# A two-layer hybrid decoder trunk on one core: mixer weights of layer 1 made ready in layer 0's feed-forward stage and kept in DRAM, and a mask added by a transfer

## The chip, the cores and the metric

The kernel runs on one core of one Trainium2 chip. Its time is the device time of one execution in microseconds (us). The profile gives, for one execution, the span from the first to the last instruction, what each engine did, and the clock that was granted to TensorE. The engines are named as in the profile: PE (TensorE matmuls), PEld (its weight loads), DVE (VectorE), ACT (ScalarE), POOL (GpSimd), SP (SyncE, which here only issues DMAs).

## The reference, cut to what matters

Two layers, each on 512 positions of width 1024, all in float32:

```python
h = rmsnorm(x, mix_pre_g[i])
z = h @ w_in[i]                      # 3206 columns: gMLP u, v | retention q, k, v, gate | FoX q, k, v, forget
...                                  # three mixers: spatial gating, retention (6 heads), forgetting attention (6 heads)
mix = concat([out_a, out_b, out_c]) @ w_o[i]
x = x + rmsnorm(mix, mix_post_g[i])
h = rmsnorm(x, ffn_pre_g[i])
g = h @ w_gate[i]                    # 1024 x 4096
act = gelu(causal_conv3(g)) * (h @ w_up[i])
x = x + rmsnorm(act @ w_down[i], ffn_post_g[i])
x = x + rmsnorm((p[i] @ w_ple_proj) * sigmoid(rmsnorm(x) @ w_ple_gate), ple_post_g[i])
```

In the forgetting attention the score of query t and key s gets the difference of two running sums of the log forget gates, and keys after the query are masked out. `log_f` is summed along the sequence by head; a row of these sums is added to the scores.

## The kernel before, in words

**Precision and the products.** A float32 matrix is cut into a high part (a cast on ACT) and a low part (the difference, on DVE); `split` does one such pair of instructions. A product then takes three matmuls on PE: high by high, high by low, low by high.

**Seven products for eight.** The feed-forward stage's gate and up projections, and 14 of the column blocks of `w_in`, are worked in pairs. Two blocks of 128 weight columns (g and u) by two halves of the contraction, against two halves of the tokens, would be eight block products; `seven` does it with seven, on sums of blocks. Each of the seven is 4 x 3 = 12 matmuls of 256 columns that go into the PSUM tiles `beta` and `ag`. `seven_weights` makes a pair ready: it loads 1 MiB into the tile `graw` (four pieces u2, u1, g1, g2 of 128x512), splits g into `wg` and u2 into `wu`, adds the pieces to each other, and splits the sums into `wsa` and `wsb`. Two of the four additions are made by DMAs that POOL issues and that add in flight, two by DVE:

```python
G.dma_start(out=u1, in_=src[:, 0, :], accum_op=ALU.add)   # u1 += u2, from DRAM
G.dma_start(out=g1, in_=src[:, 1, :], accum_op=ALU.add)   # g1 += u1, from DRAM
for t, by in ((u2, g1), (g2, u2)):                        # on DVE
    V.tensor_tensor(out=t, in0=t, in1=by, op=ALU.add)
```

The results of `seven` leave PSUM by ACT copies into `gs`/`us` (in the mixers `fqk`, `rm`, and a part of a `mix` tile) and by DVE additions. PE goes on accumulating in the same bank, so a product waits for the eviction of the one before the last.

**The stages.** For each layer: the mixers (layer 0 about 28 to 215 us, layer 1 about 808 to 985 us in the profile), the output projection, the feed-forward stage of 32 blocks of gate and up with the down projection (`dn`) woven in from block 4 (layer 0 about 250 to 723 us, layer 1 from 1030 us), and the per-layer embedding with its gate (723 to 808 us in layer 0). In a layer's mixers seven pairs are worked: three for the retention's q and k (`r0` to `r2`), three for the forgetting attention's (`f0` to `f2`), and one for two blocks of the retention's gate (`g`).

**What sets the order.** No loop of the program is the order of execution. Every instruction is recorded with its dependences; `Plan.issue` then plays the recording through with a cost for each instruction and writes down, for each engine, the order in which it would start. This order is fixed at build time. Among ready instructions the one recorded first goes first. `AHEAD` says for each stage how far ahead of the oldest unfinished instruction a tile may be taken; `STEPS` and `O_ORDER` set the order in which the mixers and the blocks of the output projection are recorded. Large tiles (8 KB in each partition) come from 24 places in two sets, 15 of `X` and 9 of `W`; `wg`, `wsa` and `wsb` live in `W`.

**The forget mask.** For a pair of heads, `fox_proj` loads a head's row of sums from DRAM to all partitions (`fcb`), and DVE makes the masked copy by adding a 128x128 mask of 0 and 1e30 to each of its four 128-column pieces. `fox_attend` uses the plain half for whole blocks and the masked half for the diagonal ones.

Of the kernel before, what the change touches and what calls it, by code (L numbers as in the profile page):

```python
# [28 lines left out]
F32 = mybir.dt.float32  # L29
# [7 lines left out]
P = 128  # L37
# [13 lines left out]
class Plan:  # L51
# [10 lines left out]
    AHEAD = {"mix": 422, "wo": 488, "wo2": 330, "emb": 950, "gu0": 403, "gu": 478, "dn": 1080, "end": 351, "pg": 618, "pg2": 206}  # L62
# [407 lines left out]
def constants():  # L470
# [16 lines left out]
    c["mask"] = np.where(idx[None, :] <= idx[:, None], 0.0, 1e30)  # L487
# [43 lines left out]
def body(ctx, tc, a, out):  # L531
# [26 lines left out]
    def b8(name, shape, dt=F32):  # L558
        kind = "W" if name in ("wg", "wsa", "wsb") else "X" if dt == F32R else None
        return b8t([P] + list(shape), dt, name, kind)  # L560
# [4 lines left out]
    def dram(name, shape):  # L565
        return dpt(list(shape), F32, tag=name, name=name, bufs=1)
# [263 lines left out]

    def seven_weights(src, dma=SUMS_BY_DMA):

# [3 lines left out]
        wg = b8("wg", (2, 1024), F32R)  # L836
# [11 lines left out]
        sa = b8("wsa", (2, 1024), F32R)  # L848
        split(sa[:, 0, :], sa[:, 1, :], raw[:, 0:1024])
        sb = b8("wsb", (2, 1024), F32R)  # L850
# [84 lines left out]
    def mixers(l, hT, uv, ready):  # L935
# [10 lines left out]
        mask = m5[:, 512:640]  # L946
        cosT = m5[:, 1536:2048]
        decay, qdec, cum, sinT = m6[:, 0:768], m6[:, 768:1152], m6[:, 1152:1408], m6[:, 1408:1920]
        for t, n in ((decay, "decay"), (qdec, "qdec"), (cum, "cum"), (mask, "mask")):
            SY.dma_start(out=t, in_=a["c_" + n])  # L950
# [95 lines left out]
        def fox_proj(p):  # L1046


            k, q = wk("fqk"), wk("fqk")
            seven(hT, seven_weights(a["w_fm"][l, 3 + p]), k, q, -0.125)  # L1050
# [44 lines left out]
        def ret_gates():  # L1095
            seven(hT, seven_weights(a["w_fm"][l, 6]), sg[:, 0, :], sg[:, 1, :])
# [6 lines left out]
        def ret_proj(p):  # L1103
            res = [wk("rm") for _ in range(2)]
            seven(hT, seven_weights(a["w_fm"][l, p]), *res)
# [138 lines left out]
    def ffn(l, hs, emb, ready, x, new, g, nxt):  # L1244
# [75 lines left out]
        for b in range(31):  # L1320
# [3 lines left out]
            gate_up(b, lambda: pieces(b))  # L1324
        plan.fence(False)
# [194 lines left out]
```

## Time and profile before

| | |
|---|---|
| time, 3 runs | 1572.74 us median (1572.61 to 1574.72) |
| the profiled execution | 1572.24 us, span 1570.5 us |
| PE | busy 1547.5 us, 10554 matmuls |
| DVE, ACT, POOL | busy 1219.3, 895.5, 229.6 us |
| DMA | 239.04 MB, of it 219.94 MB read from HBM and 17.33 MB written |

The time of the profiled execution is 1.7 us above its span. Almost all instructions come from one line (L451), because `Plan.issue` issues the recording; so the profile is read by tiles, not by lines. Busy shares are of the whole span; the stages have different limits, and what PE waits for in one of them is seen in a table by stage and in the rows of its timeline.

### The profile page before, as it was taken

To read this page: it belongs to the slowest core of one execution; us is meant where nothing else is said; L and a number is where in the kernel's file an instruction comes from. 1 tells how busy PE (TensorE), PEld (TensorE's weight loads), DVE (VectorE), ACT (ScalarE), POOL (GpSimd) and SP (SyncE) were. 2 spreads that over 40 slices of the span, in tenths; PEclk is the share of its full clock that TensorE was granted. 3 is DMA by queue.
4 is the path that set the end of the run, shared out by engine and by line. 5 is a ranking of instruction groups with operands and counts; after the bars stand their busy time and mean duration, and the time that the engine had idled before them with its cause. 6 is when DMAs were issued, how large, how long until landed. Compare 5 with 4: busy or idle time off the path is not lost. (4 is left out here: it accounts for less than half of the span.)

```text
span 1570.5 us, 27064 instructions
## 1 busy us (share of the span) xinstructions
PE 1547.5 (99%) x10554; PEld 1403.7 (89%) x10554; DVE 1219.3 (78%) x1985; ACT 895.5 (57%) x1505; POOL 229.6 (15%) x307
## 2 busy tenths in 40 slices
PE   8999999999999999999999999999999999999997
PEld 6998878999999999998889897799999999999986
DVE  6779978977778778768595699799677778778693
ACT  7548647755545545545583576586655545555462
POOL 2011023110110110102230201221011011011031
PEclk9999999999999999999999999999999999999999
DMA  9345618735644654555563546295545565464741
GB/s 331 73 121 123 239 31 251 204 95 154 153 116 130 170 131 109 166 156 206 216 162 101 122 112 202 81 287 124 158 108 155 147 164 120 121 176 100 251 165 54
DMA packets 87881, 239.04 MB, mean 152 GB/s; under 512 B 10036, under 2 KB 18364, under 8 KB 87752
## 3 DMA queue, kind: packets, MB, share of 16 engines
q1 hardware_dynamic: 64856, 195.81, 36.7%
q0 software_dynamic: 22464, 40.90, 16.1%
q8 instruction: 83, 1.36, 0.4%
q10 hardware_dynamic: 432, 0.59, 0.1%
q14 instruction: 46, 0.38, 0.1%
HBM read 219.94 MB, written 17.33 MB: 151 GB/s over the span
## 5 line engine op out<-in xcount | busy, mean ns | idle before, releaser
L451 PE MATMUL dn<-thl,act 128*128 128x512 f32 x1536 | 370.3, 391 | 0.0
L451 PEld LDWEIGHTS dn<-thl,act 128*128 128x128 f32 x1536 | 280.4, 188 | 52.3
L451 POOL DMA_DIRECT2D graw<-in_w_gu_dram x128 | 112.0, 891 | 756.7 <-DVE wg L451 470.8
L451 PE MATMUL ps<-thl,hT 128*128 128x512 f32 (+3 forms) x984 | 208.9, 368 | 0.3 <-DVE hT L451 0.3
L451 PEld LDWEIGHTS ps<-thl,hT 128*128 128x128 f32 x984 | 175.4, 188 | 24.1 <-DVE nm L451 0.8
L451 DVE TENSOR_TENSOR thl<-traw,thl 128x1024 fp32r<-128x1024 f32 (+3 forms) x124 | 141.9, 1153 | 14.1 <-ACT thl L451 13.9
L451 ACT CAST thl<-traw 128x1024 fp32r<-128x1024 f32 (+3 forms) x124 | 122.1, 1000 | 35.3 <-PE dn L451 24.1
L451 PE MATMUL beta<-hh,wu 128*128 128x256 f32 x936 | 123.1, 281 | 1.3 <-DVE us L451 1.3
L451 PEld LDWEIGHTS beta<-hh,wu 128*128 128x128 f32 x936 | 119.3, 189 | 5.6 <-DVE us L451 1.5
L451 PE MATMUL ag<-hhd,wsa 128*128 128x256 f32 x936 | 121.4, 278 | 2.7 <-DVE fqk L451 1.1
L451 DVE TENSOR_TENSOR wsb<-graw,wsb 128x1024 fp32r<-128x1024 f32 x78 | 95.3, 1221 | 35.3 <-PE beta L451 29.4
L451 PE MATMUL beta<-hh,wsa 128*128 128x256 f32 x936 | 121.1, 278 | 0.9 <-ACT gs L451 0.8
L451 PE MATMUL beta<-hh,wsb 128*128 128x256 f32 x936 | 120.1, 277 | 0.1
L451 PEld LDWEIGHTS ag<-hhd,wsa 128*128 128x128 f32 x936 | 113.0, 188 | 4.3 <-DVE gs L451 2.2
L451 DVE TENSOR_TENSOR graw<-graw 128x512 f32<-128x512 f32 x156 | 106.7, 686 | 12.9 <-DMA graw<-in_w_gu_dram 10.2
L451 PEld LDWEIGHTS beta<-hh,wsa 128*128 128x128 f32 x936 | 113.0, 188 | 2.0 <-ACT gs L451 1.5
L451 DVE TENSOR_TENSOR wg<-graw,wg 128x1024 fp32r<-128x1024 f32 x78 | 95.3, 1222 | 23.6 <-ACT wg L451 20.4
L451 PEld LDWEIGHTS beta<-hh,wsb 128*128 128x128 f32 x936 | 113.1, 188 | 0.5 <-ACT gs L451 0.3
L451 ACT CAST wsa<-graw 128x1024 fp32r<-128x1024 f32 x78 | 82.0, 1051 | 49.0 <-DVE wsb L451 25.8
L451 ACT CAST wg<-graw 128x1024 fp32r<-128x1024 f32 x78 | 82.1, 1054 | 42.3 <-PE ag L451 32.4
L451 DVE TENSOR_TENSOR wsa<-graw,wsa 128x1024 fp32r<-128x1024 f32 x78 | 95.3, 1222 | 11.7 <-ACT wsa L451 11.4
L451 DVE SCALAR_TENSOR_TENSOR cv<-gs,cw,cv 128x511 f32<-128x511 f32 (+1 forms) x128 | 95.3, 745 | 10.2 <-ACT cv L451 9.6
(220 smaller groups left out, 2677.3 us busy)
## 6 DMA issues: line engine op xcount, KB each, us to landing
graw<-in_w_gu_dram SPq DMA_DIRECT2D x128, 512.0 KB
graw<-in_w_gu_dram POOLq DMA_DIRECT2D x128, 256.0 KB, 5.6
traw<-in_w_dn_dram SPq DMA_DIRECT2D x64, 512.0 KB
x<-x SPq DMA_DIRECT2D x40, 512.0 KB
graw<-in_w_fm_dram SPq DMA_DIRECT2D x28, 512.0 KB
traw<-in_w_wo_dram SPq DMA_DIRECT2D x16, 512.0 KB
traw<-in_w_pg_dram SPq DMA_DIRECT2D x16, 512.0 KB
graw<-in_w_fm_dram POOLq DMA_DIRECT2D x28, 256.0 KB, 4.7
```

Of the source, the lines that this page charges most:

```text
L451: made = o[1](*[self.map(v) for v in o[2]], **{k: self.map(v) for k, v in o[3].items()})
```

## The change

For the seven pairs of layer 1's mixers, `keep` makes the weights ready while layer 0's feed-forward stage runs, after the recording of its blocks 5, 8, 11, 14, 17, 20 and 23, in tiles of its own (`keepwg`, `keepwsa`, `keepwsb`, and two `wu`). All four additions are on DVE there. Five stores put the result into DRAM, 3.5 MiB for a pair. In layer 1's mixers `pair_weights` loads these 3.5 MiB straight into `wg`, `wsa`, `wsb` and `wu`, where layer 0 still loads 1 MiB, adds and splits. The masked copy of a forget row is now made by a second load of the row and a DMA issued by POOL that adds the mask (128x512, four copies side by side) from DRAM; this is in both layers. `AHEAD`, `STEPS` and `O_ORDER` have new values, which act on the whole program.

```diff
-    AHEAD = {"mix": 422, "wo": 488, "wo2": 330, "emb": 950, "gu0": 403, "gu": 478, "dn": 1080, "end": 351, "pg": 618, "pg2": 206}
+    AHEAD = {"mix": 392, "wo": 1620, "wo2": 330, "emb": 291, "gu0": 480, "gu": 368, "dn": 2187, "end": 2406, "pg": 1806, "pg2": 221, "keep": 972}
...
-STEPS = "u F H f0 g f1 a0 v r0 a1 G s r1 L r2 c0 f2 a2 c1 c2"
+STEPS = "u H F f0 g f1 a0 v r0 a1 G s r2 r1 L c0 c2 f2 a2 c1"
-O_ORDER = (5, 6, 0, 1, 2, 7, 3, 4)
+O_ORDER = (5, 6, 0, 1, 2, 4, 7, 3)
+KEEP = (5, 8, 11, 14, 17, 20, 23)
...
+    def pair_weights(l, p):
+        if (l, p) not in kept:
+            return seven_weights(a["w_fm"][l, p])
+        big, wud = kept[l, p]
+        ws = [b8(n, (2, 1024), F32R) for n in ("wg", "wsa", "wsb")]
+        for t, src in zip(ws, big):
+            SY.dma_start(out=t.bitcast(F32), in_=src)
+        wu = [wk("wu", dt=F32R) for _ in range(2)]
+        for t, src in zip(wu, wud):
+            SY.dma_start(out=t.bitcast(F32), in_=src)
+        return ws[0], wu, ws[1], ws[2]
+
+    def keep(l, p):
+        wg, wu, sa, sb = seven_weights(a["w_fm"][l, p], kind="keep", dma=False)
+        big = [dram(f"k{l}_{p}_{i}", (P, 2, 1024)) for i in range(3)]
+        wud = [dram(f"ku{l}_{p}_{i}", (P, 512)) for i in range(2)]
+        for t, dst in zip((wg, sa, sb, *wu), (*big, *wud)):
+            SY.dma_start(out=dst, in_=t.bitcast(F32))
+        kept[l, p] = big, wud
...
-                SY.dma_start(out=cb[:, 0, :], in_=cums[l][2 * p + s].to_broadcast([P, S]))
-                V.tensor_tensor(out=v4(cb[:, 1, :]), in0=v4(cb[:, 0, :]), in1=mask.unsqueeze(1).to_broadcast([P, NCH, P]), op=ALU.add)
+                for i in range(2):
+                    SY.dma_start(out=cb[:, i, :], in_=cums[l][2 * p + s].to_broadcast([P, S]))
+                G.dma_start(out=cb[:, 1, :], in_=a["c_mask"], accum_op=ALU.add)
...
+            if l + 1 < DEPTH and b in KEEP:
+                plan.stage = "keep"
+                keep(l + 1, KEEP.index(b))
+                plan.stage = "gu"
```

The matmuls are the same 10292 after the idle ones at the start, by tile and size, in both kernels, and so is the number of places (269) at which one kind of matmul gives way to another; only their order is new. What moves is on DVE, ACT, SP and POOL. Three places show it. A name's number tells the tile apart; `graw` is a raw pair, `in_w_gu_dram` the weights of gate and up, `in_w_fm_dram` those of the mixers, `k1_1_0` to `k1_1_2` and `ku1_1_0`, `ku1_1_1` the kept tiles of layer 1's pair 1.

DVE early in layer 0's feed-forward stage, about two blocks, before:

```order
L451 TENSOR_TENSOR wsb_4125<-graw_3879,wsb_4125 128x1024
L451 TENSOR_TENSOR gs_4079<-ag_4061,gs_4079 128x256
L451 TENSOR_TENSOR wg_4153<-graw_4022,wg_4153 128x1024
L451 SCALAR_TENSOR_TENSOR cv_4162<-gs_4079,cw_2838,cv_4162 128x511
L451 TENSOR_TENSOR facc_3536<-dn_4151,facc_3536 128x512
L451 SCALAR_TENSOR_TENSOR cv_4162<-gs_4079,cw_2838,cv_4162 128x510
L451 TENSOR_TENSOR graw_3924<-graw_3924 128x512 x2
L451 TENSOR_TENSOR wu_4207<-graw_4159,wu_4194 128x512
```

and now:

```order
L451 TENSOR_TENSOR gs_4108<-ag_4105,gs_4108 128x256
L451 TENSOR_TENSOR keepwsa_4114<-graw_3759,keepwsa_4114 128x1024
L451 TENSOR_TENSOR keepwsb_4127<-graw_3759,keepwsb_4127 128x1024
L451 TENSOR_TENSOR graw_3847<-graw_3847 128x512
L451 TENSOR_TENSOR wsa_4140<-graw_3847,wsa_4140 128x1024
L451 SCALAR_TENSOR_TENSOR us_4164<-beta_4087,us_4164 128x256
L451 TENSOR_TENSOR wg_4179<-graw_4062,wg_4179 128x1024
L451 TENSOR_TENSOR gs_4108<-ag_4105,gs_4108 128x256
```

Between the evictions `gs` and `us` of one block now stand two splits of a kept pair, beside the addition and the split of a block's own weights.

SP in the same stretch, where before only loads of `graw` and `traw` follow each other, now:

```order
L451 DMA traw_3693<-in_w_dn_dram 128x1024 x2
L451 DMA graw_3759<-in_w_fm_dram 128x1024 x2
L451 DMA graw_3847<-in_w_gu_dram 128x1024 x2
L451 DMA ku1_1_0_3875<-wu_3865 128x512
L451 DMA ku1_1_1_3880<-wu_3873 128x512
L451 DMA k1_1_0_4056<-keepwg_4037 128x2048
L451 DMA graw_4062<-in_w_gu_dram 128x1024 x2
L451 DMA traw_4085<-in_w_dn_dram 128x1024 x2
L451 DMA k1_1_1_4154<-keepwsa_4114 128x2048
L451 DMA k1_1_2_4172<-keepwsb_4127 128x2048
L451 DMA graw_4183<-in_w_gu_dram 128x1024 x2
```

The load of a block's weights (`graw_4062`, `graw_4183`) now stands behind stores that wait for DVE's split of a kept tile.

SP ahead of layer 1's mixers, before:

```order
L451 DMA traw_8272<-in_w_fv_dram 128x2x390 x2
L451 DMA x2_8288<-x_8066 128x1024 x2
L451 DMA traw_8358<-in_w_fv_dram 128x2x390 x2
L451 DMA graw_8411<-in_w_fm_dram 128x1024 x2
L451 DMA x2_8288<-x_8080 128x1024
L451 DMA graw_8526<-in_w_fm_dram 128x1024 x2
L451 DMA x2_8288<-x_8080 128x1024
L451 DMA graw_8624<-in_w_fm_dram 128x1024 x2
```

and now:

```order
L451 DMA wu_8635<-ku1_3_0_4893 128x512
L451 DMA x2_8502<-x_8315 128x1024
L451 DMA wu_8653<-ku1_3_1_4905 128x512
L451 DMA wg_8668<-k1_3_0_4929 128x2048
L451 DMA wsa_8712<-k1_3_1_5060 128x2048
L451 DMA wsb_8744<-k1_3_2_5105 128x2048
L451 DMA x2_8502<-x_8315 128x1024
L451 DMA wg_8808<-k1_6_0_6488 128x2048
L451 DMA wsa_8817<-k1_6_1_6724 128x2048
L451 DMA wsb_8822<-k1_6_2_6738 128x2048
```

For the first three pairs six loads of 512 KiB have become fifteen of together 10.5 MiB (some of them follow further on), and they go straight into the tiles that PE reads.

More of the change, by code (lines that the diff above doesn't have):

```diff
@@ L558, in b8 @@
     def b8(name, shape, dt=F32):
-        kind = "W" if name in ("wg", "wsa", "wsb") else "X" if dt == F32R else None
+        kind = None if name.startswith("keep") else "W" if name in ("wg", "wsa", "wsb") else "X" if dt == F32R else None
         return b8t([P] + list(shape), dt, name, kind)
@@ L1104, in ret_proj @@
             res = [wk("rm") for _ in range(2)]
-            seven(hT, seven_weights(a["w_fm"][l, p]), *res)
+            seven(hT, pair_weights(l, p), *res)
             for m in res:
```

22 lines of the change are left out of this document (11 added, 11 removed).

## The prediction

> **What bounds the kernel now.** I read the page's busy line first, then the chain of waits, then a table by stage, and at last PE's timeline in the stage that the change relieves.
>
> ```profile
> span 1570.5 us, 27064 instructions
> PE 1547.5 (99%) x10554; PEld 1403.7 (89%) x10554; DVE 1219.3 (78%) x1985; ACT 895.5 (57%) x1505; POOL 229.6 (15%) x307
> ```
>
> PE is idle for 1570.5 - 1547.5 = 23 us in all. Busy is not yet full speed, so the chain must say at what pace the products run:
>
> ```profile
> 808.07 23.94 PE ps L451 x126
> ...
> 834.74 1.36 PE beta L451 x12
> ...
> 844.38 1.41 PE ag L451 x12
> ...
> 1204.93 1.42 PE beta L451 x12
> ...
> 1219.99 1.42 PE beta L451 x12
> ```
>
> A product of twelve matmuls takes 1.36 or 1.41 us. The feed-forward stage repeats every 1219.99 - 1204.93 = 15.06 us, which is seven products (7 x 1.36 = 9.5) and 24 `dn` matmuls (5.5 us): PE alone sets this pace. Then the stages:
>
> ```profile
> core 0: us, PE busy (x) PEld busy (x) DVE busy (x) ACT busy (x) POOL busy (x), PEclk, DMA share, GB/s
> 60.00:215.00 155.00, 153.55 (x1152) 136.12 (x1151) 127.14 (x327) 92.54 (x174) 20.68 (x22) 1.00 0.47 135
> 215.00:310.00 95.00, 91.85 (x631) 83.38 (x630) 82.13 (x121) 63.83 (x117) 22.34 (x34) 1.00 0.67 194
> 310.00:723.00 413.00, 411.61 (x2928) 383.80 (x2928) 313.11 (x427) 218.75 (x332) 41.84 (x48) 1.00 0.53 143
> 723.00:808.00 85.00, 84.16 (x401) 69.11 (x401) 64.27 (x86) 53.27 (x99) 28.96 (x43) 1.00 0.56 187
> 808.00:985.00 177.00, 175.45 (x1264) 157.26 (x1263) 143.72 (x346) 103.99 (x193) 21.01 (x24) 1.00 0.47 131
> 985.00:1030.00 45.00, 43.80 (x213) 35.77 (x213) 33.67 (x48) 27.93 (x57) 14.59 (x25) 1.00 0.44 138
> 1030.00:1075.00 45.00, 44.77 (x382) 44.37 (x381) 44.15 (x65) 35.46 (x58) 7.86 (x9) 1.00 0.87 261
> 1075.00:1490.00 415.00, 414.57 (x2971) 387.55 (x2970) 314.13 (x431) 220.00 (x335) 42.67 (x49) 1.00 0.53 143
> ```
>
> Layer 1's mixers are 808 to 985 us: PE is idle 177.00 - 175.45 = 1.55 us there. DVE is busy 143.72 of 177 us, and that is work which PE covers. So the stage that loses the most DVE work has 1.55 us of PE waits to give. They are almost all in three rows of PE's timeline:
>
> ```profile
> 860.43 1.69 PE L451 MATMUL ag<-hT,wsb 128*128 128x256 f32 x12 [0.51 <-ACT fqk L451]
> ...
> 892.34 1.69 PE L451 MATMUL ag<-hhd,wsa 128*128 128x256 f32 x12 [0.48 <-DVE rm L451]
> ...
> 945.60 1.65 PE L451 MATMUL ag<-hhd,wsa 128*128 128x256 f32 x12 [0.47 <-DVE fqk L451]
> ```
>
> Each is a product that goes on accumulating and waits for the eviction of its bank, which is late on ACT or DVE: 0.51 + 0.48 + 0.47 = 1.46 us.
>
> **The change part by part. Layer 1's mixers.** The durations:
>
> ```profile
> L451 DVE TENSOR_TENSOR graw<-graw 128x512 f32<-128x512 f32 x156 | 106.7, 686 | 12.9 <-DMA graw<-in_w_gu_dram 10.2 <-DMA graw<-in_w_fm_dram 1.3
> ...
> L451 DVE TENSOR_TENSOR wsb<-graw,wsb 128x1024 fp32r<-128x1024 f32 x78 | 95.3, 1221 | 35.3 <-PE beta L451 29.4 <-ACT wsb L451 5.9
> ...
> L451 ACT CAST wsa<-graw 128x1024 fp32r<-128x1024 f32 x78 | 82.0, 1051 | 49.0 <-DVE wsb L451 25.8 <-PE ag L451 16.1 <-DVE graw L451 5.8
> ...
> L451 DVE TENSOR_TENSOR wu<-graw,wu 128x512 fp32r<-128x512 f32 x78 | 53.4, 685 | 11.0 <-ACT wu L451 10.9
> ...
> L451 ACT CAST wu<-graw 128x512 fp32r<-128x512 f32 x78 | 48.4, 620 | 16.4 <-DMA graw<-in_w_gu_dram 13.5 <-DMA graw<-in_w_fm_dram 2.8
> ...
> L451 DVE TENSOR_TENSOR fcb<-fcb,mix 128x512 f32<-128x512 f32 x12 | 8.2, 686 | 1.6 <-DMA fcb<-cums 1.6
> ```
>
> A pair takes 3 x 1.221 + 0.685 + 2 x 0.686 = 5.72 us of DVE and 3 x 1.051 + 0.620 = 3.77 us of ACT; seven pairs 40.0 and 26.4 us. With six mask additions of 0.686 us, DVE sheds 44 of its 144 us (a few splits start before 808 us). The long instructions behind which the late evictions stand are mostly these. I take the three stalls as gone: **-1.5 us**. Bounds: 0, if other long instructions take their place, and -1.55. The pace can add to it: 49 products at 1.36 or 1.41 us, 49 x 0.05 = 2.4 us either way; the rows do not say what sets it, so I take 0.
>
> What PE then waits for in this stage could be DMA. By the queues:
>
> ```profile
> q1 hardware_dynamic: 64856, 195.81, 36.7%
> q0 software_dynamic: 22464, 40.90, 16.1%
> ```
>
> q1 moved 195.81 MB in 0.367 x 1570.5 = 576 us of all engines, 340 GB/s; q0, POOL's adding transfers, 40.90 MB in 253 us, 162 GB/s. Seven pairs of 3.67 MB add 75.6 us; seven loads of 1.05 MB (21.6 us) and seven times 0.52 MB of adding transfers (22.7 us) go; the masks bring 6 x 0.26 MB on each queue, 4.6 + 9.7 us. Net 46 us in 177: the share goes from 0.47 to 0.73. The three pairs at the start need 11 MB, 32 us; SP issues them from about where it issued their `graw` before, and PE has 24 us of `ps` work from 808 us on (the row at 808.07) ahead of the first product. I take 0, bounds 0 to 3 us (the third pair late by 10%).
>
> **Layer 0's feed-forward stage** gets the work: per pair 3 x 1.221 + 0.685 + 4 x 0.686 = 7.09 us of DVE, since all four additions are on it, together 49.7 us, and 26.4 us of ACT. In 310 to 723 us DVE goes from 313.1 to 363 of 413 us (76 to 88%), ACT from 218.8 to 245 (53 to 59%). DMA gets seven times 1.05 + 3.67 MB, 33 MB or 97 us: its share goes from 0.53 to 0.53 + 97/413 = 0.77. What hides all this is PE's 15.06 us a block; without that cover it would be worth 50 us. The nearest row is 1030 to 1075 us, with DVE at 44.15/45 = 98% and DMA at 0.87, and PE idle 0.23 of 45 us, 0.5%. The stage now loses 1.39 of 413, 0.3%. For the 19 blocks in which pairs are made, 286 us, the difference is 0.6 us: I take **+0.5 us**. The upper bound is the worst stretch, 215 to 310 us, with 3.15 of 95 us idle, 3.3%: 9.5 us. The lower is -1.4, all that is idle there now.
>
> On SP, stores wait for DVE's splits and the loads of later blocks stand behind them. What SP waits for today:
>
> ```profile
> SPq L451 <- PE ag L451: 313.2, 54, 20.2
> SPq L451 <- DVE wsb L451: 281.7, 26, 16.6
> ```
>
> SP mostly waits for places to come free, up to 20 us at a time, so loads run well ahead and some of that is spent on stores: 0.
>
> **The masks.** A 0.686 us addition becomes a second load and an adding transfer:
>
> ```profile
> L451 DVE CUSTOM_DVE_ANT_0 pe<-sps,fcb x48: 272/348/558, 91.6 to 967.5; 128x128 f32<-128x128 f32 x24, 128x256 f32<-128x256 f32 x12, 128x384 f32<-128x384 f32 x12
> ...
> L451 DVE TENSOR_TENSOR fcb<-fcb,mix x12: 681/685/693, 78.8 to 928.9; 128x512 f32<-128x512 f32 x12
> ```
>
> The first masked row is made at 78.8 us and first read at 91.6, 12.8 us later; such transfers land in 4.7 us (rows below). Hidden: 0; without that slack up to 4 us for each of six pairs of heads.
>
> **The new orders.** `AHEAD`, `STEPS` and `O_ORDER` act everywhere. Idle PE elsewhere between 60 and 1490 us is 1.45 + 3.15 + 0.84 + 1.20 + 0.23 + 0.43 = 7.3 us. I take a small part, **-0.5 us**; bounds -7.3 and as much the other way.
>
> **Sum.** -1.5 + 0.5 - 0.5 = -1.5 us. The profiled execution took 1572.24 us, 1.7 above its span and 0.5 below the median; against the median 1572.74 - 1.5 = **1571.2 us**.
>
> **The rivals.** *Faster: the new orders close the gaps between stages.* 7.3 + 1.4 + 1.5 = 10.2 us of waits are within their reach; at half, 1572.7 - 5.1 = 1567.6 us. For it: a relieved DVE leaves room to place evictions. Against: 3.15 of it lies in 215 to 310 us, where DVE is at 86% with work that the change does not touch.
>
> *Slower: DVE stands behind a late transfer.* It has happened once already:
>
> ```profile
> 292.02 1.65 PE L451 MATMUL beta<-hh,wu 128*128 128x256 f32 x12 [1.27 <-DVE us L451]
> ...
> 290.28 0.69 DVE L451 TENSOR_TENSOR graw<-graw 128x512 f32<-128x512 f32 x1 [1.78 <-DMA graw<-in_w_gu_dram]
> ...
> graw<-in_w_gu_dram POOLq DMA_DIRECT2D x6, 256.0 KB, 7.8
> ...
> graw<-in_w_gu_dram POOLq DMA_DIRECT2D x33, 256.0 KB, 5.5
> ...
> graw<-in_w_fm_dram POOLq DMA_DIRECT2D x8, 256.0 KB, 4.7
> ```
>
> DVE waited at a `graw` addition for POOL's adding transfer, the eviction `us` stood behind it, and PE lost 1.27 us. The last three rows give the landing in 250 to 280 us (DMA share 0.99), 400 to 660 us, and 808 to 985 us. If the stores fill the queues as in the first, and each of seven pairs costs one such stall, 7 x 1.27 = 8.9 us: 1572.7 + 8.9 - 1.5 = 1580 us. It decides once landings go from 5.5 towards 7.8 us over the 286 us. Against it: at 0.87 (1030 to 1075 us) PE lost only 0.23 us. [...]
>
> [...]
>
> *Hidden anyway: the three stalls are replaced by others.* 1572.7 us.
>
> **How the numbers follow.** About 0.2%, 3.1 us, is what can be told from no change: faster is below 1569.6 us, slower above 1575.9. Forecast 0.39 (own range, by the pace, 1568.8 to 1573.6), hidden anyway 0.10, faster rival 0.32, late transfers 0.16, starved mask 0.03. The forecast's edge puts 0.03 of its chance below 1569.6: faster 0.35, same 0.46, slower 0.19. The range of 8 in 10 leaves out the far ends, nearly all the waits gone on the one side and most of the late transfers on the other: 1566.0 to 1577.0 us.
>
> **What would show it.** Right: in layer 1's mixers DVE falls by some 40 us while PE stays within 1 us of full; in layer 0's feed-forward stage DVE is near 88%, DMA near 0.77, blocks still 15.06 us apart. Wrong: PE rows there with idle time that ends with DVE `gs` or `us` or with a DMA; PE waits for `wg`, `wsa` or `wu` from DRAM at the first three pairs; or idle time between the stages that has shrunk by several us.

## The result and the profile after

The changed kernel is **slower**: 1589.3 us (median of four runs, 1584.7 to 1590.0) against 1572.8 (1572.6 to 1574.7). The ratio is 1.0096 (95% interval 1.0075 to 1.0116), 16.5 us at the medians. The forecast was 1571.2 us, range 1566 to 1577.

The profiled execution took 1584.68 us and is the fastest of the four, so its trace holds about 12 of the 16.5 us. Its page:

```profile
span 1583.0 us, 27228 instructions
PE 1552.0 (98%) x10554; PEld 1404.2 (89%) x10554; DVE 1214.9 (77%) x1987; ACT 895.3 (57%) x1505; POOL 226.5 (14%) x305
...
q1 hardware_dynamic: 76376, 250.21, 45.3%
q0 software_dynamic: 22176, 40.38, 15.3%
```

PE is idle for 1583.0 - 1552.0 = 31 us where it was 23, and busy 4.5 us longer with the same 10554 matmuls. SP's queue (q1) moves 250 MB where it moved 196. The table by stage follows, with each stretch cut where the work of the old stretch begins and ends (the old 60, 215, 310, 723, 808 and 985 us are 60, 222, 319, 739, 823 and 997 here):

```profile
core 0: us, PE busy (x) PEld busy (x) DVE busy (x) ACT busy (x) POOL busy (x), PEclk, DMA share, GB/s
60.00:222.00 162.00, 155.99 (x1151) 137.03 (x1150) 121.17 (x317) 90.94 (x171) 24.60 (x26) 0.99 0.51 145
222.00:319.00 97.00, 93.10 (x633) 84.04 (x631) 87.27 (x128) 66.57 (x119) 22.25 (x35) 1.00 0.65 188
319.00:739.00 420.00, 413.90 (x2929) 384.65 (x2928) 350.98 (x481) 243.95 (x361) 43.55 (x50) 1.00 0.71 221
739.00:823.00 84.00, 83.68 (x400) 69.05 (x399) 61.70 (x82) 50.67 (x97) 23.87 (x40) 1.00 0.58 207
823.00:997.00 174.00, 173.50 (x1259) 155.21 (x1257) 105.31 (x300) 80.61 (x165) 16.10 (x18) 1.00 0.65 225
```

Layer 1's mixers did what they were to do: 174 us instead of 177, 0.5 us idle instead of 1.55, DVE 105 us instead of 144. The loss lies in layer 0: its mixers take 162 us instead of 155, its feed-forward stage 420 instead of 413. And the clock, 1.00 in every row before, is 0.99 in the first.

A finer measure is used from here on. By tile and size, the traces of all kernels have the same 10554 matmuls (16 idle ones at the start and 10538 others), so the start of the matmul that stood at a boundary in the kernel before can be read in every trace; the difference, less that at the boundary before it, is what a stage gained or lost. (Inside the mixers the order of matmuls differs between kernels, so a boundary there is good to about 1 us.) The last column goes from the start of the span to the last matmul. In us, for the runs told below:

| kernel, profiled run | 60-215: layer 0's mixers | 215-310: into its feed-forward | 310-723: feed-forward | 723-808 | 808-985: layer 1's mixers | 985-1490: into and through its feed-forward | whole |
|---|---|---|---|---|---|---|---|
| changed | 7.0 | 1.9 | 6.9 | -0.7 | -2.1 | -0.3 | 12.8 |
| tables alone | 3.6 | 1.7 | 1.5 | -0.1 | 2.5 | -1.0 | 8.5 |
| mask alone | 4.8 | 0.6 | 0.1 | 0.0 | 5.5 | 1.9 | 13.1 |
| kept pairs alone | -0.6 | 0.1 | 20.1 | -0.7 | 1.6 | 2.9 | 24.0 |
| changed without kept pairs | 7.0 | 2.5 | 0.0 | 0.0 | 4.1 | -0.3 | 13.6 |
| changed, mask on DVE | 3.1 | 1.5 | 7.5 | -0.7 | -2.9 | 1.7 | 10.7 |
| mask in the old order | 5.6 | 0.8 | 1.2 | 0.0 | 5.1 | -0.4 | 12.7 |
| kept pairs, other numbers | -0.4 | -0.8 | 4.5 | -0.9 | -1.0 | 3.0 | 4.2 |
| order nudged by 2% | 4.5 | 0.1 | -0.2 | -0.1 | -1.0 | 4.3 | 7.7 |

Five of PE's waits in the changed kernel, from its timeline (start, duration, what; in brackets the idle time ahead of it and what ended it):

```profile
90.69 1.65 PE L451 MATMUL beta<-hh,wu 128*128 128x256 f32 x12 [1.06 <-DVE fqk L451]
...
123.19 2.51 PE L451 MATMUL beta<-hh,wsa 128*128 128x256 f32 x10 [0.97 <-DVE wsa L451]
...
322.56 1.42 PE L451 MATMUL beta<-hh,wsa 128*128 128x256 f32 x10 [1.11 <-DVE wsa L451]
...
447.35 1.65 PE L451 MATMUL ag<-hhd,wsa 128*128 128x256 f32 x12 [1.76 <-DVE gs L451]
...
676.66 1.64 PE L451 MATMUL beta<-hh,wsa 128*128 128x256 f32 x12 [1.93 <-ACT gs L451]
```

Two things are to be seen. The waits end with a split (`wsa`) or an eviction (`gs`), that is with ACT's or DVE's queue, never with a load of the kept weights. And ten matmuls at 123.19 take 2.51 us where twelve take 1.5: half speed (the clock is 0.50 or 0.51 from 123.0 to 126.0 us). What stood ahead of `gs` at 447 is in DVE's timeline, and ahead of `gs` at 677 in ACT's:

```profile
442.61 1.22 DVE L451 TENSOR_TENSOR keepwg<-graw,keepwg 128x1024 fp32r<-128x1024 f32 x1 [2.36 <-ACT keepwg L451]
...
446.88 0.42 DVE L451 TENSOR_TENSOR gs<-ag,gs 128x256 f32<-128x256 f32 x1
```

```profile
672.17 1.05 ACT L451 CAST thl<-traw 128x1024 fp32r<-128x1024 f32 x1 [3.30 <-DMA traw<-in_w_dn_dram]
```

DVE stood 2.36 us at a kept pair's split, and then had 4.3 us of queue ahead of the eviction that PE needed. ACT stood 3.30 us at a split whose load was late, with the eviction behind it. The wait at 90.69 us comes up again with the mask.

### The profile page after: what moved, and what is told of

The parts are those of the page before. It is cut to its first block, busy times and chain, and to the rows that moved or that the text cites. A ratio compares the mean times of both kernels' runs of the same rounds, so it can differ in the third digit from the quotient of the medians.

```text
span 1583.0 us, 27228 instructions
## 1 busy us (share of the span) xinstructions
PE 1552.0 (98%) x10554; PEld 1404.2 (89%) x10554; DVE 1214.9 (77%) x1987; ACT 895.3 (57%) x1505; POOL 226.5 (14%) x305
## 4 chain that ended last, share of the span: by engine, by line
PE 69%; DVE 7%; DMA 4%; issue 2%; ACT 1%; POOL 1%; SPq 0%; DVEq 0%; POOLq 0%; ACTq 0%
PE dn L451 20%; PE beta L451 20%; PE ag L451 15%; PE ps L451 9%; DMA graw<-in_w_gu_dram 1%; PE wo L451 1%; DVE cv L451 1%; DVE graw L451 1%; DMA traw<-in_w_dn_dram 1%; PE hps L451 1%; DMA graw<-in_w_fm_dram 1%; DMA traw<-in_w_rv_dram 1%; PE sps L451 1%; DVE wsa L451 1%; DVE thl L451 1%
## 5 line engine op out<-in xcount | busy, mean ns | idle before, releaser
L451 DVE TENSOR_TENSOR graw<-graw 128x512 f32<-128x512 f32 x170 | 115.5, 684 | 11.8 <-DMA graw<-in_w_gu_dram 10.3
L451 ACT CAST wsa<-graw 128x1024 fp32r<-128x1024 f32 x71 | 74.6, 1051 | 51.8 <-PE ag L451 28.4
L451 PEld LDWEIGHTS beta<-hb,wg 128*128 128x128 f32 x768 | 96.8, 188 | 5.8 <-DVE wg L451 0.8
L451 DVE TENSOR_TENSOR wsa<-graw,wsa 128x1024 fp32r<-128x1024 f32 x71 | 86.6, 1220 | 18.5 <-ACT wsa L451 17.9
L451 PE MATMUL beta<-hb,wg 128*128 128x256 f32 x768 | 99.7, 277 | 0.7 <-DVE wg L451 0.7
L451 DVE TENSOR_TENSOR wg<-graw,wg 128x1024 fp32r<-128x1024 f32 x71 | 86.5, 1219 | 17.5 <-ACT wg L451 15.1
```

The costliest lines, as they stand in the source:

```text
L451: made = o[1](*[self.map(v) for v in o[2]], **{k: self.map(v) for k, v in o[3].items()})
```

## The experiments

**One part at a time.** First each of the three parts alone on the kernel before.

```diff
 tables_alone: the kernel before, but
-AHEAD = {"mix": 422, "wo": 488, ...}   STEPS = "u F H f0 ..."   O_ORDER = (5, 6, 0, 1, 2, 7, 3, 4)
+AHEAD = {"mix": 392, "wo": 1620, ...}  STEPS = "u H F f0 ..."   O_ORDER = (5, 6, 0, 1, 2, 4, 7, 3)
 mask_alone: the changed kernel with the old three tables and KEEP = ()
 keep_alone: the changed kernel with the old three tables and the mask added on DVE
 keep_mask_old_tables: the changed kernel with the old three tables
```

> The kernel before with only the new AHEAD, STEPS and O_ORDER; no kept pairs, mask added on DVE. The changed kernel lost 12.5 us of span: some 7 us up to 310 us (layer 0's mixers, out-projection, entry to the feed-forward stage), some 6 us in layer 0's feed-forward stage. If the orders lose the first 7 us: 1578 to 1581 us, with the stalls before 310 us there again and the feed-forward stage as before (1.4 us idle). If they are harmless, as the prediction had it: 1571 to 1574 us. If orders are worth a few us either way by chance (any new order lands somewhere within +-5 us): anything from 1568 to 1578.

> The kernel before with only the forget mask added by POOL's transfer; old tables, no kept pairs. In the changed kernel this transfer took 9.6 us to land (the median of four between 60 and 130 us) beside 4.4 us for the adding transfers of weights there. If the late mask is what loses the 7 us before 310 us: 1576 to 1580 us, and PE or DVE rows that wait for fcb. If it is hidden (prediction): 1571.5 to 1573.5 us.

> The kernel before with only the seven pairs kept (old tables, with the new entry keep: 972; mask on DVE). If the kept pairs lose the 6 us in layer 0's feed-forward stage whatever the orders: 1576 to 1580 us, that stage with some 5 to 7 us idle, the mixers of layer 1 with 0.8 us idle, layer 0's mixers as before. If the loss there comes from the new AHEAD: 1571 to 1574 us. As the prediction had it: 1571.7 us.

> The changed kernel with the old AHEAD, STEPS and O_ORDER (keep: 972 stays). If the losses add up part by part, this is the changed kernel's 1589 less what the new tables alone cost; by the theory that the tables lose the first 7 us: 1578 to 1582 us. If the mask transfer or the kept pairs lose all: 1585 to 1590 us.

Measured, with the ratio's interval: tables alone 1580.1 us (1.0025 to 1.0059), mask alone 1584.8 (1.006 to 1.009), kept pairs alone 1599.3 (1.0156 to 1.019), both with the old tables 1613.6 (1.0227 to 1.029); before 1573.2. **Each part alone costs, and the mask and the kept pairs cost far more with the old tables than with the new, as the next two runs show.** The first time is where the theory of harmful orders had it; the other three are above every theory. The new tables lose 6.8 us by themselves, but on top of the two other parts they win 24 (40.4 us over before against 16.5): they fit this kernel, the old ones the old. The page of the tables alone shows two parts in their loss:

```profile
PE 1552.4 (98%) x10554; PEld 1405.6 (89%) x10554; DVE 1218.5 (77%) x1985; ACT 892.7 (57%) x1505; POOL 232.0 (15%) x307
```

PE is idle for 1578.6 - 1552.4 = 26.2 us, 3.2 more than before, and busy 4.9 us longer with the same matmuls, though the clock is 1.00 up to 1498 us. So the larger part is not waits but the pace of the products; no run shows what sets it.

Then one part taken out of the changed kernel.

```diff
 changed_without_keep
-KEEP = (5, 8, 11, 14, 17, 20, 23)
+KEEP = ()
 changed_mask_on_dve
-G.dma_start(out=cb[:, 1, :], in_=a["c_mask"], accum_op=ALU.add)     (and the second load of the row)
+V.tensor_tensor(out=v4(cb[:, 1, :]), in0=v4(cb[:, 0, :]), in1=mask..., op=ALU.add)
```

> The changed kernel without the kept pairs (mask by transfer, new tables). If the kept pairs lose what the trace shows in layer 0's feed-forward stage (6 us) and gain 0.7 us in layer 1's mixers: 1582 to 1585 us. If any other order is worse than the one the tables were chosen with: 1585 to 1595 us. If the kept pairs cause nearly all of it: 1574 to 1579 us.

> The changed kernel with the mask added on DVE as before (kept pairs, new tables). If the mask transfer loses the 7 us up to 310 us: 1580 to 1584 us, with no wait of PE at 90 and 122 us. If the new orders lose them: 1586 to 1592 us.

Measured 1585.3 us (1.0061 to 1.0099) and 1582.8 (1.0047 to 1.0086); before, beside them, 1572.3. Each median against that of before in the same series: tables alone +6.8, with the mask +13.0, with the kept pairs too +16.5. So the steps are **6.8 for the tables, 6.2 for the mask, 3.5 for the kept pairs**; with the kept pairs put in before the mask it is 6.8 for the tables, 3.7 for the kept pairs and 6.0 for the mask. The stage table says where. The whole loss of the feed-forward stage belongs to the kept pairs (6.9 with them, 0.0 without), and they give back 6.2 in layer 1's mixers (-2.1 against 4.1). The mask transfer costs nearly 4 of the 7.0 in layer 0's mixers (7.0 against 3.1); the tables hold the rest.

**Is it the order?** The kernel before, every number of `AHEAD` up by 2%, nothing else:

> The kernel before with every number of AHEAD raised by 2% and nothing else: the same work in a slightly other order. If the order that stands in the kernel before is one of many equal ones: 1572 to 1575 us. If it is a lucky one, and any new order costs some us through waits at places that nobody looked at: 1576 to 1586 us; then the 6.9 us of the new tables alone and most of the 11.6 us of the mask alone are of this kind and tell nothing about the operations themselves.

Measured 1578.0 us (1.0013 to 1.0034). So, as far as one nudge can tell, the order of the kernel before is a lucky or a chosen one: a change that adds no work costs 4 us (in the table its profiled run has 7.7, of them 4.5 in layer 0's mixers and 4.3 after 985 us). Some of the tables' 6.8 us may be of this kind; no run tells how much. To cost an operation, the order must therefore be held fixed. The next runs do that: the planner lays out the old instructions, and only what is issued in their place differs.

**The mask with the order fixed.** PE, ACT and DVE run exactly as before; DVE's twelve additions are gone, and POOL's transfers stand at their places in the plan.

```diff
 in the planner's last loop (mask_in_old_order), with PE, ACT and DVE in the order of before
-SP: row -> cb0                       DVE: cb1 = cb0 + mask
+SP: row -> cb0, row -> cb1           POOL: cb1 += mask (DMA)
```

> The kernel before with PE, ACT and DVE in exactly its order; only the twelve mask additions leave DVE's queue, and in their place in the plan stand twelve adding transfers in POOL's queue; the second load of the row goes right behind the first in SP's. If the transfer itself is hidden, as the prediction had it (landing 8.6 us, slack 12.8 us at the first): 1571 to 1575 us, and the 11.6 us of the mask alone come from the order that the planner then made. If the late landing or the place in POOL's queue costs PE: 1576 to 1586 us, with PE or DVE rows behind fcb at 92 to 100 us and at the later pairs of heads.

Measured 1584.0 us (1.0047 to 1.0094): 11.7 us over before, as much as the mask alone with an order of its own (11.6). The prediction's cover did not hold. Two waits, one in each layer, are nearly all of it, and ACT's timeline says why. PE's rows, then ACT's ahead of the first:

```profile
91.47 2.46 PE L453 MATMUL beta<-hh,wsb 128*128 128x256 f32 x12 [4.37 <-ACT fqk L453]
...
870.55 2.93 PE L453 MATMUL beta<-hh,wsb 128*128 128x256 f32 x12 [4.33 <-ACT fqk L453]
```

```profile
86.75 0.83 ACT L453 CAST thl<-traw 128x768 fp32r<-128x768 f32 x1 [3.47 <-DMA traw<-in_w_rv_dram]
90.31 0.83 ACT L453 CAST thl<-traw 128x768 fp32r<-128x768 f32 x1 [2.74 <-DMA traw<-in_w_rv_dram]
91.05 0.37 ACT L453 COPY fqk<-beta 128x256 f32<-128x256 f32 x1
```

At these two places PE does not wait for the mask. It waits for the eviction `fqk`, which stands in ACT's queue behind two splits of `w_rv` (the weights of the retention's v), and these wait for their loads. In the kernel before, ACT ran the same two splits without idle time ahead of them:

```profile
82.93 1.57 ACT L451 CAST thl<-traw 128x768 fp32r<-128x768 f32 x2
```

SP issues the loads of `w_rv` right behind the rows, and four more rows and four adding transfers are now in the queues with them. In the stretches of this kernel the DMA share (the column before the last) is above 1.0 there, where it was 0.46 from 80 to 100 us before, and the clock falls behind the wait:

```profile
88.00:90.00 2.00, 0.00 (x0) 0.00 (x0) 0.57 (x1) 0.00 (x0) 0.88 (x1) 1.00 1.11 263
90.00:92.00 2.00, 0.53 (x4) 0.53 (x5) 0.82 (x1) 1.39 (x3) 0.00 (x0) 1.00 1.08 338
92.00:94.00 2.00, 2.00 (x12) 2.00 (x12) 0.14 (x1) 1.38 (x2) 0.00 (x0) 0.51 1.05 353
94.00:96.00 2.00, 2.00 (x13) 2.00 (x13) 1.29 (x2) 0.64 (x2) 0.00 (x0) 0.63 0.77 206
```

For 4 us after the wait PE has a clock (the column behind POOL's) of 0.51 and 0.63, some 1.7 us lost again (2 x 0.49 + 2 x 0.37). A wait thus costs 4.4 + 1.7 = 6 us, and two of them, 12 us, are the 11.7 measured.

The changed kernel itself shows the same chain at 90 us. ACT stood at a split of `w_rv`, DVE at its half of that split, and the eviction `fqk` for which PE waited 1.06 us stood behind it in DVE's queue:

```profile
88.48 0.84 ACT L451 CAST thl<-traw 128x768 fp32r<-128x768 f32 x1 [1.56 <-DMA traw<-in_w_rv_dram]
```

```profile
89.34 0.96 DVE L451 TENSOR_TENSOR thl<-traw,thl 128x768 fp32r<-128x768 f32 x1 [5.04 <-ACT thl L451]
90.22 0.42 DVE L451 SCALAR_TENSOR_TENSOR fqk<-beta,fqk 128x256 f32<-128x256 f32 x1
```

Two runs take the fixed order apart.

```diff
 mask_rows_only: as mask_in_old_order, but
-POOL: cb1 += mask (DMA)              (left out; the rows are still loaded twice)
 mask_rows_after_rv: as mask_in_old_order, but (POOL's adding transfers move with the second rows)
-SP: rows -> cb0, cb1;  w_rv x4
+SP: rows -> cb0;  w_rv x4;  rows -> cb1
```

> The mask in the old order, but the twelve adding transfers are left out (the rows are loaded twice, the mask is not added, so that part of the output is left wrong); PE, ACT and DVE in the order of before. With the transfers PE lost 4.4 us at 91 and 4.3 us at 871, each time with ACT at a split that waited for the loads of w_rv (3.5 and 2.7 us) and the eviction fqk behind it, and then 3.4 us at half clock: 11.7 us in all. If the traffic holds back w_rv: the second rows alone (1 MB a layer) still cost something, the adding transfers (1 MB more) the rest: 1574 to 1580 us, with shorter waits at the same two places. If the place of the adding transfers in POOL's queue is the cause: no waits there, 1572 to 1574 us.

> The mask in the old order with all its transfers, but the second load of the first four rows (of three of four in layer 1) stands behind the four loads of w_rv in SP's queue, and POOL's adding transfers behind these. If late loads of w_rv are the cause: no PE wait for fqk at 91 and 871 and 1573 to 1578 us; a new wait for the mask may show, since its adding transfers then land some 5 us later, behind the first score at 91.6. If the masks themselves were what PE waited for: 1584 us or more.

Measured 1578.3 us (1.0023 to 1.0049) and 1584.5 (1.0051 to 1.0087). With the second rows alone PE's same two products wait less:

```profile
88.09 1.68 PE L453 MATMUL beta<-hh,wsb 128*128 128x256 f32 x12 [1.63 <-ACT fqk L453]
...
864.99 2.10 PE L453 MATMUL beta<-hh,wsb 128*128 128x256 f32 x12 [3.20 <-ACT fqk L453]
```

So traffic ahead of `w_rv` is the cause, as expected, and nearly half of the price (5.4 of 11.7 us) is the plain second load. With `w_rv` first, the wait for `fqk` at 91 us is gone, which bears this out, but the time is not: now DVE waits for the mask, and PE for DVE.

```profile
96.50 0.29 DVE L462 CUSTOM_DVE_ANT_0 pe<-sps,fcb 128x128 f32<-128x128 f32 x1 [5.32 <-DMA fcb<-in_c_mask_dram]
```

```profile
96.85 2.07 PE L462 MATMUL sps<-fqk 64*128 64x512 f32 x2 [3.24 <-DVE nm L462]
```

Behind this wait the clock is 0.50 from 96 to 102 us. The expectation of 1573 to 1578 us was wrong: whichever of the two goes second is late. (At 868 us, where one second row still goes first, a wait of 1.05 us for `fqk` is left, and short ones for the scores follow, with a clock of 0.50 from 878 to 880 us.) How long the mask takes, from the answers on the tile and on the queues of the changed kernel (60 to 130 us for the second line):

```profile
DMA to landing us min/median/max: 7.4/9.6/11.3
```

```profile
graw<-in_w_fm_dram POOLq DMA_DIRECT2D x6, 256.0 KB, 4.4
```

An adding transfer of the same 256 KB lands in 4.4 us for weights and in 9.6 for the mask. Whether that is its kind or its place was not taken apart; with `w_rv` first (`mask_rows_after_rv`) the mask's land in 4.1 to 8.2 us, median 6.8.

**The kept pairs with the order fixed.** In the kept pairs alone, nearly all of the 20 us in the feed-forward stage are two waits of PE, 13.4 us, and the slower clock behind them (0.55, 0.50 and 0.81 in the stretches of 3 us from 440 us; 0.67, 0.50 and 0.69 from 569). DVE's timeline around the first follows them:

```profile
442.67 0.80 PE L451 MATMUL beta<-hh,wsa 128*128 128x256 f32 x2 [7.13 <-ACT wsa L451]
...
572.66 0.80 PE L451 MATMUL beta<-hh,wsa 128*128 128x256 f32 x2 [6.22 <-ACT wsa L451]
```

```profile
436.00 0.42 DVE L451 TENSOR_TENSOR gs<-ag,gs 128x256 f32<-128x256 f32 x1 [0.70 <-PE ag L451]
436.34 1.22 DVE L451 TENSOR_TENSOR keepwg<-graw,keepwg 128x1024 fp32r<-128x1024 f32 x1
437.47 0.68 DVE L451 TENSOR_TENSOR wu<-graw,wu 128x512 fp32r<-128x512 f32 x1
438.07 4.79 DVE L451 TENSOR_TENSOR graw<-graw 128x512 f32<-128x512 f32 x7
442.78 1.22 DVE L451 TENSOR_TENSOR wsa<-graw,wsa 128x1024 fp32r<-128x1024 f32 x1
```

PE ends its product at 435.5 and next needs `wsa`. The additions for it stand in DVE's queue behind the eviction `gs` of that very product, a kept pair's split, another split, and four additions of the kept pair (four of the seven in the row at 438.07). Is it the bytes of the stores, or DVE's work? With the order untouched, the stores of six pairs were cut to 16 columns, and in a second run the DVE and ACT work of these pairs too.

```diff
 keep_small_stores: keep_alone, six of seven pairs
-SY.dma_start(out=dst, in_=t)
+SY.dma_start(out=dst[..., 0:16], in_=t[..., 0:16])
 keep_hollow: as well, every DVE and ACT instruction of these pairs on [..., 0:16]
```

> The kept pairs alone (old tables) in exactly the same order on PE, DVE, ACT and POOL, but for six of the seven pairs the five stores write 16 columns of each row in place of all (0.05 MB in place of 3.67), and layer 1 loads pair 0's weights seven times, the same number of bytes; that part of the output is therefore left wrong. Kept pairs alone ran 1599.3 us; its profile has PE waits of 7.1 us (442) and 6.2 us (572), each behind a DMA share of 1.0 over the 25 us before. If the stores' bytes hold back loads and adding transfers: both waits gone, 1575 to 1582 us. If it is the added DVE work or its place in the queue: both stay, 1593 to 1600 us.

> The kept pairs alone (old tables), same order on every engine, but for six of seven pairs the DVE and ACT instructions of a kept pair work on 16 columns instead of 512 or 1024, and its stores write 16 (layer 1 loads pair 0's weights seven times; that part of the output is left wrong). The loads stay whole. With small stores and whole DVE work the time was 1594.6 us, with PE waits of 7.1 us (441) and 4.7 us (571), in front of which DVE ran a kept pair's split and four additions (0.7 + 1.2 + 0.7 + 4 x 0.68 = 5.3 us) before the three additions that PE's next product needed. If the DVE work of the kept pairs is the cause: these waits shrink to under 2 us and the time falls to 1574 to 1582 us. If it is the order in which DVE waits for data (its own loads, whatever DVE does with them): waits of 4 to 6 us stay, 1586 to 1593 us.

Measured 1594.6 us (1.0119 to 1.0154) and 1590.8 (1.0094 to 1.0135). Without the stores' bytes, and then without the work as well, PE still waits at the same products:

```profile
441.35 0.80 PE L451 MATMUL beta<-hh,wsa 128*128 128x256 f32 x2 [7.13 <-ACT wsa L451]
...
571.41 0.50 PE L451 MATMUL beta<-hh,wsa 128*128 128x256 f32 x2 [4.69 <-ACT wsa L451]
```

```profile
438.08 0.79 PE L451 MATMUL beta<-hh,wsa 128*128 128x256 f32 x2 [3.81 <-ACT wsa L451]
...
567.21 0.50 PE L451 MATMUL beta<-hh,wsa 128*128 128x256 f32 x2 [4.69 <-ACT wsa L451]
```

Over before, in their own series, the three runs stand at 26.0, 21.0 and 18.5 us: by the medians the stores' bytes are 5 of the 26, the DVE and ACT work 2.5, and 18.5 are left with both gone. The profiled runs divide it otherwise. They stand at 23.2, 23.7 and 17.9 us over the profiled run of before, with 20.1, 20.1 and 16.3 of it in the feed-forward stage; the price of the bytes is not seen in them. In both readings 16 us or more are left. DVE's rows ahead of the first wait in `keep_hollow` show what these are:

```profile
434.37 0.42 DVE L451 TENSOR_TENSOR gs<-ag,gs 128x256 f32<-128x256 f32 x1 [0.78 <-PE ag L451]
434.83 0.17 DVE L451 TENSOR_TENSOR keepwg<-graw,keepwg 128x16 fp32r<-128x16 f32 x1
434.94 0.69 DVE L451 TENSOR_TENSOR wu<-graw,wu 128x512 fp32r<-128x512 f32 x1
435.54 2.73 DVE L451 TENSOR_TENSOR graw<-graw 128x16 f32<-128x16 f32 x7
438.19 1.22 DVE L451 TENSOR_TENSOR wsa<-graw,wsa 128x1024 fp32r<-128x1024 f32 x1
```

(Of the seven additions four are a kept pair's, on 16 columns, and three the block's own.) From `gs` on DVE is never idle, so no load is late here. The additions that PE needs next stand behind an eviction that must itself wait for PE, so the wait is written into DVE's queue; the kept pair's work in between only made it longer (7.13 us with it, 3.81 without). At the second wait no instruction of a kept pair stands in between, and it is 4.69 us both with small stores and here. The two waits, 8.5 us, and the clock behind them (0.67, 0.50 and 0.69 in the stretches of 3 us from 437 us; 0.79, 0.50 and 0.57 from 566) are nearly all of the 16.3 us. If the order is the cause, another one with all the work and all the bytes must lose it. A first attempt ranked a kept pair's instructions later in the planner:

```diff
 keep_as_background (old tables, mask on DVE) and changed_as_background (the changed kernel)
-heapq.heappush(waiting[o[0]], (at, i, i))
+heapq.heappush(waiting[o[0]], (at, i + 1500 * (self.stages[i] == "keep"), i))
```

> The kept pairs alone (old tables), but the planner ranks the instructions of a kept pair 1500 places later than the program order has them, so that an instruction of the next blocks that is ready goes first on each queue. If the loss comes from a kept pair's instructions standing ahead of work that PE waits for next: 1575 to 1584 us, no PE wait over 3 us in layer 0's feed-forward stage. If the stores' bytes are the cause: the DMA share stays as high and the time at 1592 to 1602 us.

> The changed kernel (new tables, mask by transfer) with the same later rank for the kept pairs' instructions. The changed kernel lost 6 us in layer 0's feed-forward stage, of 16.5 in all at the median. If rank is what loses them: 1582 to 1585 us. If not, or if the new order costs as much elsewhere: 1587 to 1593 us.

Measured 1596.3 us (1.0127 to 1.0166) and 1593.3 (1.0112 to 1.0161): no help. In both profiles no wait of PE in the feed-forward stage is over 2.3 us, but there are more than ten, together 13.1 and 9.8 us where the kernel before has 1.4. (1596.3 lies where the stores' bytes were expected to put it; the run with small stores limits these to 5 us.) The second attempt changed numbers only; they were found by letting the planner lay out many sets and taking the one that it had end earliest.

```diff
 keep_other_numbers: keep_alone (seven pairs, all work, all bytes, STEPS and O_ORDER of before), but
-AHEAD = {"mix": 422, "wo": 488, "wo2": 330, "emb": 950, "gu0": 403, "gu": 478, "dn": 1080, "end": 351, ...}
+AHEAD = {"mix": 422, "wo": 488, "wo2": 379, "emb": 484, "gu0": 806, "gu": 420, "dn": 2160, "end": 357, ...}
 keep_three_pairs: three pairs only, KEEP = (6, 13, 20), AHEAD again chosen so
```

> The kept pairs alone, whole, with other numbers in AHEAD (mix 422, wo 488, wo2 379, emb 484, gu0 806, gu 420, dn 2160, end 357, pg 216, pg2 175, keep 826) and the old STEPS and O_ORDER. Kept pairs alone with the old numbers ran 1599.3 us; with their DVE and ACT work and their stores hollowed out in the same order still 1590.8. If the order that the numbers make is what costs: 1577 to 1584 us, no PE wait over 3 us in layer 0's feed-forward stage. If the kept pairs' own traffic and DVE work cost it: 1590 to 1600 us.

> Only three pairs kept (the fox pairs 3 to 5, in blocks 6, 13 and 20), the others made in layer 1 as before; AHEAD mix 422, wo 501, wo2 379, emb 465, gu0 394, gu 484, dn 513, end 201, pg 635, pg2 393, keep 3127, the old STEPS and O_ORDER, mask on DVE. A version that might beat the kernel before: the stalls at 860 and 946 belong to these pairs. If less kept work costs less: 1571 to 1577 us. If any other order than that of before costs some 4 us, whatever is kept: 1575 to 1580 us.

Measured 1575.9 us (1.0013 to 1.0034) and 1574.5 (1.0002 to 1.0026). **The same seven pairs cost 26 us in one order and 3 in another**, less than either theory expected. So some 23 of the 26 us were the order. Their price with a fair order can be read from two stretches of keep_other_numbers:

```profile
310.00:723.00 413.00, 409.06 (x2903) 380.57 (x2902) 344.58 (x474) 233.67 (x351) 43.51 (x50) 1.00 0.72 221
...
808.00:985.00 177.00, 176.58 (x1269) 156.79 (x1268) 109.80 (x306) 84.05 (x170) 10.26 (x11) 1.00 0.60 210
```

PE is idle for 3.9 us in the feed-forward stage (1.4 before) and 0.4 in layer 1's mixers (1.55 before). That is +2.5 and -1.1; the stage table, which counts the pace of the products too, has 4.5 and -1.0.

**A version that beats both?** Each pair one block later, or three pairs only, again with numbers of their own.

```diff
 keep_seven_later: KEEP = (6, 9, 12, 15, 18, 21, 24), AHEAD chosen for it; mask on DVE, old STEPS and O_ORDER
 keep_three_later: KEEP = (9, 15, 21) for the fox pairs, AHEAD chosen for it; mask on DVE, old STEPS and O_ORDER
```

> All seven pairs kept, mask on DVE, old STEPS and O_ORDER, each pair one block later (6, 9, ... 24) and other numbers in AHEAD (mix 422, wo 486, wo2 397, emb 484, gu0 765, gu 456, dn 2160, end 303, pg 216, pg2 166, keep 357). With one earlier set of numbers the seven pairs ran 1575.9 us: layer 1's mixers 1.1 us better than before in PE waits, layer 0's feed-forward stage 2.5 us worse. If the numbers can take the waits out of the feed-forward stage: 1570 to 1573 us, faster than before by up to 2 us. If DVE at 83% in that stage always leaves some: 1574 to 1577 us.

> Three pairs kept (the fox pairs, in blocks 9, 15 and 21), mask on DVE, old STEPS and O_ORDER, AHEAD mix 422, wo 501, wo2 379, emb 465, gu0 509, gu 381, dn 256, end 266, pg 444, pg2 412, keep 3127. The earlier version with three pairs ran 1574.5 us, with one PE wait of 2.1 us at 527. If that wait goes: 1571 to 1573 us. If another takes its place: 1574 to 1576 us.

Measured 1574.9 us (0.9996 to 1.0015), no difference, and **1570.9 (0.9966 to 0.9988), faster than before by 0.23%**, 2.9 us. The second is the best of four such versions, so a part of its gain may be luck of the choice. No run gives the old work numbers chosen in the same way, so it is not shown that the kept pairs make the gain and not the new numbers. Its profiled execution, 1572.5 us, is one of its slower ones; the gain is in the times and not seen in that trace.

## Why the prediction was wrong

The prediction's sum was -1.5 us: -1.5 + 0.5 for the kept pairs, 0 for the masks, -0.5 for the new orders. The runs gave +16.5: 3.5 for the kept pairs, 6.2 for the masks, 6.8 for the orders. So the masks and the orders, which it took as nothing and as a small gain, are 13.5 of the 18 us missed.

**Layer 1's mixers, -1.5: right.** PE's idle time fell by 1.05 us and the stage by 2.1; the rest is in the pace, for which the prediction left 2.4 either way and took 0, or in the 1 us to which this boundary is good. DVE sheds 38 us there (144 to 105) where 40 to 44 were counted. The three pairs at the start are not late: no wait of PE ends with a load of kept weights.

**Layer 0's feed-forward stage, +0.5: the mechanism named, its size wrong.** It lost 6.9 us, inside the stated bounds of -1.4 to 9.5. The busy shares came out near the forecast (DVE 351 of 420 us, 84% where 88 was said; DMA 0.71 where 0.77), so the mean load did not mislead; the step that failed is the nearest row. A stretch of 45 us with DVE at 98% that loses 0.5% shows that a full queue in a good order loses little; it says nothing of another order. The same work cost this stage 4.5 us in one order and 20.1 in another. One of the signs of being wrong that the prediction gave, PE rows there whose idle time ends with `gs` on DVE, is what the profile shows (447.35).

**The rival of late adding transfers: right place, other cause.** It put 7 x 1.27 us on adding transfers that land late. They land in 6.0 us in this stage against 5.0 before (medians of 50 and 48), short of the 7.8 that the rival needed, and in the kept pairs alone cutting the stores' bytes with the order fixed left both long waits. DVE did stand at the wrong instruction, but at a kept pair's split and in the planned order.

**The masks, 0: the step that failed.** With every order fixed the transfer costs 11.7 us, and 6.2 on top of the new tables. The prediction counted the mask's own slack, 12.8 us from the first masked row to its first read, and a landing of 4.7 us. The landing was 7 to 11, still inside it. What it left out is the other loads in the queues: with the order fixed `w_rv`, issued right behind the rows, came late, ACT stood at its split, and the eviction behind that held PE for 4.4 us, once in each layer. The 0.03 for a starved mask was for the mask itself coming late. Nor is the slack enough once `w_rv` goes first: DVE then waits 5.3 us for the mask, whose second load and adding transfer start later (POOL issues the first at 88.98 us, in `mask_in_old_order` at 79.02). How the 6.2 us of the changed kernel divide is seen only in part. The wait at 90.69 us is of this kind; the two at 121 to 123 us are also gone when the mask is added on DVE, but their chain begins with DVE at another load (3.12 us at 118.90, for `in_sgu_v_g_dram`), and why that came late is open.

**The new orders, -0.5: wrong sign.** Alone they cost 6.8 us, inside the bounds of 7.3 either way. For the term itself the prediction gave no reason but the idle time elsewhere, of which it took a small part as something to win; "a relieved DVE leaves room", the argument of its faster rival, does not hold for the tables alone, which relieve nothing. Idle time was also the wrong thing to count: of the 8 us that the profiled run of the tables alone lost, 3.2 are idle time and 4.9 the pace, which the prediction left open for layer 1's mixers only and took as 0. A nudge by 2% costs 4 us too, so the order before seems to be better than those near it. What sets the pace stays open.

Not settled: the three other runs of the changed kernel took some 4.6 us more than the profiled one, and no trace shows where.

## What to carry to other kernels

A transfer that is hidden by its own slack need not be free (the mask's, with 12.8 us of slack, cost 11.7 us with the order held): list every load that stands behind it in the queues, and for each the engine that will stand at it and the eviction that is queued behind. In a kernel whose order is searched, an edit and its order are one change; cost the operation with the order held fixed, and the order by running the old work in a nudged one. When moved work costs more than it should, cut its bytes and its instructions in place before blaming load: here 18.5 of 26 us stayed, and another order took away most of them.

## What was not expected of the hardware

A wait of PE can cost more than its length. After 4.4 us idle the twelve matmuls at 91.47 took 2.46 us instead of 1.58, with a granted clock of 0.51; after 7.1 us in the kept pairs alone ten took 2.50, with a clock of 0.50. The changed kernel has one such stretch after two gaps of 0.8 and 1.0 us (its stretches from 120 us on):

```profile
120.00:122.00 2.00, 1.21 (x11) 0.68 (x11) 2.00 (x6) 1.53 (x2) 0.87 (x1) 1.00 0.47 94
122.00:124.00 2.00, 1.03 (x6) 0.94 (x6) 2.00 (x2) 0.98 (x2) 0.00 (x0) 0.75 0.86 264
124.00:126.00 2.00, 2.00 (x11) 2.00 (x11) 1.98 (x14) 1.32 (x3) 0.86 (x1) 0.50 1.09 302
126.00:128.00 2.00, 2.00 (x17) 2.00 (x17) 1.48 (x4) 1.84 (x9) 0.00 (x0) 0.89 0.74 114
```

The clock column falls to 0.75, 0.50 and 0.89: 3.4 us at half clock if it is read as half or full (1.0 + 2.0 + 0.4; in stretches of 0.5 us it is 0.50 or 0.51 from 123.0 to 126.0, 0.58 in the next, and 1.00 in the others from 120 to 129), some 1.7 us lost, as much as the two gaps. The kernel before has a clock of 1.00 in every stretch between 60 and 1490 us. Not every wait does this: in the mask alone a wait of 2.40 us at 175.88 has it behind (0.73, 0.50 and 0.92 in the stretches of 2 us from 176 us; twelve matmuls took 2.06 us), one of 2.26 us at 385.86 in `changed_as_background` has not (the twelve matmuls at 388.39 took 1.52). Of the longer waits in the rows above, the one of 4.37 us has a clock of 0.51 behind it and the one of 3.24 a clock of 0.50; behind 4.33 us twelve matmuls took 2.93 us, behind 3.20 the twelve at 866.89 took 2.71, and behind the 7.13 and 6.22 us of the kept pairs alone and the 3.81 and 4.69 of `keep_hollow` ten took 2.50. In the changed kernel PE was busy for 2.2 of the 4 us from 120 us on (1.21 + 1.03), so there the lower clock came behind two gaps and not behind one long wait. No run shows what sets it. The prediction priced waits by their length alone.
